# Copies for shuffles and a later iota in a sliding-window kernel bound by DMA

## The chip, the cores and the metric

One core of one Trainium2 chip. The time is the device time of one execution in microseconds (us). The kernel before takes 190.28 us (median of 3 runs, 190.25 to 190.29). The span of a profile, from its first to its last instruction, is about 1.7 us shorter than the time.

## The reference, cut to what matters

```python
# x: (16, 64, 64, 64) float32, window_size 8, stride 4  ->  n_h = n_w = 15
for i in range(n_h):
    for j in range(n_w):
        result[:, i, j] = x[:, :, 4*i:4*i+8, 4*j:4*j+8]     # (16, 64, 8, 8) each
```

It computes nothing: every window is copied out. The input has 16.8 MB, the output 3600 windows of 16 KB, 59 MB.

## The kernel before

The input stays in SBUF as `L`: 128 partitions, each one half of the channels of one batch element and one band of 16 image rows (4 bands). A tile `G` collects 128 windows of 16 KB, one in a partition, by copies of ScalarE and VectorE; GpSimd then scatters its rows to the output by an indirect DMA. Four `G` buffers rotate. A **crossing unit** fills one half of the partitions with windows that lie within a band (`s` = 2) and the other half with windows that cross into the next band (`s` = 3). The last band has no crossing windows, so 16 of the 128 rows fall outside the output and are dropped.

```python
    def fill(g, half, s, j, lo, n, copies):
        ...
            if s < NSLOT - 1:
                copy(out=g[d, cs, :, :], in_=L[f, :, s * ST : s * ST + WS, cols])
            else:
                copy(out=g[d, cs, 0:ST, :], in_=L[f, :, s * ST : RB, cols])
                nc.vector.stream_shuffle(out=g[d, cs, ST:WS, :], in_=L[f, :, 0:ST, cols], mask=nxt)

    def shf(out, in_):                       # an identity shuffle: a plain move
        nc.vector.stream_shuffle(out=out, in_=in_, mask=same)

    def mix(out, in_):
        k = out.shape[1] // 4
        act(out=out[:, 0:k], in_=in_[:, 0:k])
        shf(out=out[:, k:], in_=in_[:, k:])
    ...
            turn = crossed % 2               # in unit(), for s > 0
            crossed += 1
            fill(g, turn, s, j, 0, HP, (act, act))
            fill(g, 1 - turn, s + 1, j, 0, HP, (shf, mix))
            scatter(g, (idx_hi, idx_lo)[turn], j, s)
```

`turn` decides which half of the partitions gets the crossing windows. The iota and the index arithmetic stand ahead of the loads. At the end, two half tiles (the last column of windows) leave by DMAs of SyncE and ScalarE.

Of the kernel before, what the change touches and what calls it, by code (L numbers as in the profile page):

```python
# [10 lines left out]
def kernel(  # L11
# [7 lines left out]
    nc = tc.nc  # L19
    P = nc.NUM_PARTITIONS  # L20

    B, C, H, W = x.shape
# [8 lines left out]
    CH = 2  # L31
    HQ = P // (B * CH)
    CL = C // CH
# [4 lines left out]
    HP = P // CH  # L38
    YB = 8
    NY = B // YB  # L40
# [8 lines left out]
    L = lpool.tile([P, CL, RB, W], f32)  # L49
# [4 lines left out]
    SMALL, HWP = 4, 8  # L54

    def load(eng, ch, y, q, c0, c1):
        p0 = ch * HP + y * QP + q
        eng.dma_start(out=L[p0 : p0 + QP - HQ + 1 : HQ, c0:c1, :, :], in_=x_v[ch, y, q, :, c0:c1, :])  # L58
# [3 lines left out]
    def itile(name):  # L62
        return ipool.tile([P, 1], i32, name=name)

    pi, tb, tq, tc_, th, idx, idx_y0, idx_y1, idx_lo, idx_hi = (
        itile(n) for n in ("pi", "tb", "tq", "tc", "th", "idx", "idx_y0", "idx_y1", "idx_lo", "idx_hi")
    )
    FAR = float(2 * B * NWIN)
    nc.gpsimd.iota(pi[:, :], pattern=[[0, 1]], base=0, channel_multiplier=1)  # L69

    def bits(d, shift, mask):
        nc.vector.tensor_scalar(out=d[:, :], in0=pi[:, :], scalar1=shift, scalar2=mask, op0=ALU.logical_shift_right, op1=ALU.bitwise_and)  # L72
# [4 lines left out]
    def tt(d, a, b, op):  # L77
        nc.vector.tensor_tensor(out=d[:, :], in0=a[:, :], in1=b[:, :], op=op)  # L78
# [20 lines left out]
    tt(idx_lo, tb, th, ALU.add)  # L99
    mul(th, tc_, NW)  # L100
    tt(idx_lo, idx_lo, th, ALU.add)


    EC = 8
    x_b = x.rearrange("b (ch cl) (hq r) w -> ch hq b cl (r w)", ch=CH, hq=HQ)
    nc.scalar.dma_start(out=L[HP : HP + (B - 1) * HQ + 1 : HQ, 0:EC, :, :], in_=x_b[1, 0, :, 0:EC, :])

    for y in range(NY):
        for q in range(HQ):
            hw = y * HQ + q < HWP  # L110
            if hw:
                load(nc.sync, 0, y, q, SMALL, CL)
            load(nc.gpsimd, 0, y, q, 0, SMALL if hw else CL)
            load(nc.gpsimd, 1, y, q, EC if q == 0 else 0, CL)

    o_v = out.rearrange("b i j c r w -> (b i j) (c r w)")
    nxt = [min(p + 1, 31) for p in range(32)]
# [9 lines left out]
    def scatter(g, ix, j, s):  # L127
        st = nc.gpsimd.indirect_dma_start(  # L128
            out=o_v,
            out_offset=bass.IndirectOffsetOnAxis(ap=ix[:, 0:1], axis=0),  # L130
            in_=g.rearrange("p c r w -> p (c r w)"),
            in_offset=None,
            element_offset=(s * NW + j) * CFREE,
            bounds_check=B * NWIN - 1,
            oob_is_err=False,
        )
        free(st)

    def fill(g, half, s, j, lo, n, copies):

        d = slice(half * HP + lo, half * HP + lo + n)
        cols = slice(j * ST, j * ST + WS)
        for ch in (half, 1 - half):
            f = slice(ch * HP + lo, ch * HP + lo + n)
            cs = slice(ch * CL, (ch + 1) * CL)
            copy = copies[ch != half]
# [6 lines that stand above are left out]
    act, dve = nc.scalar.copy, nc.vector.tensor_copy  # L153
    same = list(range(32))


    def shf(out, in_):
        nc.vector.stream_shuffle(out=out, in_=in_, mask=same)  # L158

    def mix(out, in_):  # L160
        k = out.shape[1] // 4
        act(out=out[:, 0:k], in_=in_[:, 0:k])  # L162
        shf(out=out[:, k:], in_=in_[:, k:])


    EARLY = 3
# [2 lines left out]
    def tile_():  # L169
        nonlocal at  # L170
        at += 1
        return G[(at - 1) % NG]
# [16 lines left out]
    def unit(j, s, fast=False):  # L189
        nonlocal crossed  # L190
        g = tile_()
        if s == 0:
            fill(g, 0, 0, j, 0, HP, (act, dve if fast else shf))
            fill(g, 1, 1, j, 0, HP, (act, dve if fast else mix))
            scatter(g, idx, j, s)
        else:

            turn = crossed % 2
            crossed += 1
            fill(g, turn, s, j, 0, HP, (act, act))  # L200
            fill(g, 1 - turn, s + 1, j, 0, HP, (shf, mix))
            scatter(g, (idx_hi, idx_lo)[turn], j, s)

    for n in range(EARLY):
# [3 lines left out]
    for n in range(EARLY):  # L208
        part(1, 2 * n)
        unit(*plain.pop(0), fast=True)  # L210
    while plain:
        for w in cross[:3]:
            unit(*w)
        cross = cross[3:]
        unit(*plain.pop(0))


    j = NW - 1
    tile_()
    for s in range(2):  # L220
        g = tile_()
# [44 lines left out]
```

## Time and profile before

| | before |
|---|---|
| time, median | 190.28 us |
| VectorE, ScalarE, GpSimd busy | 75%, 74%, 25% |
| DMA, mean over the span | 401 GB/s |
| stores by GpSimd | 29, issued from 43 to 173 us |
| last crossing store lands; last DMA lands | 177.5 us; 187.6 us |

From the page: the summary by engine, then two rows of 40 slices (DMA share in tenths, GB/s), then one DMA queue (packets, MB, share of 16 engines).

```profile
DVE 142.5 (75%) x200; ACT 139.2 (74%) x89; POOL 46.9 (25%) x50
...
DMA  4999999999999999999999999999999999999993
GB/s 118 308 409 397 402 401 397 397 403 394 427 434 420 435 434 416 434 434 413 437 437 408 439 430 420 423 437 416 427 413 434 428 409 430 406 437 378 427 389 153
...
q14 instruction: 4, 0.03, 0.0%
```

DMA is full from the second slice to the last but one. The row `q14` looks like nothing: four packets of 8 KB, on a queue that the page calls `instruction`.

### The profile page before, as it was taken

To read this page: it belongs to the slowest core of one execution; us is meant where nothing else is said; L and a number is where in the kernel's file an instruction comes from. 1 tells how busy PE (TensorE), PEld (TensorE's weight loads), DVE (VectorE), ACT (ScalarE), POOL (GpSimd) and SP (SyncE) were. 2 spreads that over 40 slices of the span, in tenths; PEclk is the share of its full clock that TensorE was granted. 3 is DMA by queue.
4 is the path that set the end of the run, shared out by engine and by line. 5 is a ranking of instruction groups with operands and counts; after the bars stand their busy time and mean duration, and the time that the engine had idled before them with its cause. 6 is when DMAs were issued, how large, how long until landed. Compare 5 with 4: busy or idle time off the path is not lost.

```text
span 189.0 us, 557 instructions
## 1 busy us (share of the span) xinstructions
DVE 142.5 (75%) x200; ACT 139.2 (74%) x89; POOL 46.9 (25%) x50
## 2 busy tenths in 40 slices
DVE  4000009999697979799989999999999999997410
ACT  0000009998699999988889999999999999974740
POOL 7321212207217170522220222222222222223000
DMA  4999999999999999999999999999999999999993
GB/s 118 308 409 397 402 401 397 397 403 394 427 434 420 435 434 416 434 434 413 437 437 408 439 430 420 423 437 416 427 413 434 428 409 430 406 437 378 427 389 153
DMA packets 11044, 75.81 MB, mean 401 GB/s; under 512 B 3344, under 2 KB 3344, under 8 KB 7440
## 3 DMA queue, kind: packets, MB, share of 16 engines
q0 software_dynamic: 8784, 65.81, 84.0%
q1 hardware_dynamic: 2048, 8.91, 12.0%
q10 hardware_dynamic: 208, 1.05, 1.8%
q14 instruction: 4, 0.03, 0.0%
HBM read 16.78 MB, written 62.91 MB: 422 GB/s over the span
## 4 chain that ended last, share of the span: by engine, by line
DMA 66%; DVE 18%; issue 6%; ACT 3%; POOL 2%; DVEq 0%; ACTq 0%; PEldq 0%
DMA out_dram<-G,idx_hi 24%; DMA L<-in_x_dram 23%; DMA out_dram<-G,idx 13%; DVE G L158 10%; DMA out_dram<-G,idx_y 7%; DVE G L151 5%; DVE G L181 3%; ACT G L227 2%; POOL L L58 2%; ACT G L148 1%; DVE G L148 0%; DVEq L181 0%; POOL pi L69 0%; DVEq L158 0%; PEldq L261 0%
## 5 line engine op out<-in xcount | busy, mean ns | idle before, releaser
L148 ACT COPY G<-L 64x2048 f32<-64x2048 f32 x46 | 87.2, 1896 | 5.5 <-DMA out_dram<-G,idx 2.3
L181 DVE COPY G<-L 32x2048 f32<-32x2048 f32 x30 | 36.6, 1221 | 29.3 <-DMA L<-in_x_dram 26.7
L158 DVE STREAM_SHUFFLE G<-L 64x1024 f32<-64x1024 f32 (+3 forms) x40 | 55.7, 1392 | 1.3
L151 DVE STREAM_SHUFFLE G<-L 64x1024 f32<-64x1024 f32 x30 | 38.5, 1282 | 0.0
L181 ACT COPY G<-L 32x2048 f32<-32x2048 f32 x18 | 33.9, 1896 | 2.9 <-DMA L<-in_x_dram 2.3
L181 ACT ACT_TABLE_LOAD x1 | 1.3, 1283 | 28.3 <-DMA L<-in_x_dram 28.3
L58 POOL DMA_DIRECT2D L<-in_x_dram x16 | 10.9, 691 | 23.0 <-DMA L<-in_x_dram 22.5
L128 POOL DMA_INDIRECT out_dram<-G,idx_y x6 | 10.0, 1664 | 25.5 <-DVE G L181 24.5
L128 POOL DMA_INDIRECT out_dram<-G,idx x8 | 11.3, 1412 | 19.9 <-DVE G L158 6.5
L128 POOL DMA_INDIRECT out_dram<-G,idx_hi x8 | 7.7, 963 | 30.7 <-DVE G L151 23.1
L128 POOL DMA_INDIRECT out_dram<-G,idx_lo x7 | 6.7, 961 | 27.5 <-DVE G L151 19.1
L227 ACT COPY G<-L 32x2048 f32<-32x2048 f32 x4 | 7.6, 1896 | 5.1 <-DMA out_dram<-G,idx_lo 4.0
L162 ACT COPY G<-L 64x256 f32<-64x256 f32 (+1 forms) x20 | 9.1, 456 | 0.5
L227 DVE COPY G<-L 32x2048 f32<-32x2048 f32 x4 | 4.9, 1219 | 3.5 <-DMA out_dram<-G,idx_hi 2.4
L148 DVE COPY G<-L 64x2048 f32<-64x2048 f32 x6 | 7.3, 1222 | 0.2
L158 DVE LOAD_MASK_SELECT G<-L x40 | 0.4, 9 | 2.1 <-DMA out_dram<-G,idx_y 1.2
L72 DVE TENSOR_SCALAR tb<-pi 128x1 int32<-128x1 int32 x1 | 0.2, 153 | 1.0 <-POOL pi L69 1.0
L78 DVE TENSOR_TENSOR th<-tc,tq 128x1 int32<-128x1 int32 x2 | 0.3, 156 | 0.0
L75 DVE TENSOR_SCALAR th<-tc 128x1 int32<-128x1 int32 x2 | 0.3, 154 | 0.0
L69 POOL IOTA pi<- 128x1 int32 x1 | 0.1, 124 | 0.4 <-PEq L261 0.4
L151 DVE LOAD_MASK_SELECT G<-L x30 | 0.2, 7 | 0.0
L78 DVE CUSTOM_DVE_ANT_0 idx_lo<-tb,th 128x2 uint16<-128x2 uint16 x1 | 0.2, 159 | 0.0
(18 smaller groups left out, 2.6 us busy)
## 6 DMA issues: line engine op xcount, KB each, us to landing
L<-in_x_dram SPq DMA_DIRECT2D x8, 896.0 KB
L<-in_x_dram POOLq DMA_DIRECT2D x6, 1024.0 KB, 21.6
L<-in_x_dram POOLq DMA_DIRECT2D x2, 768.0 KB, 18.3
out_dram<-G SPq DMA_DIRECT2D x6, 256.0 KB
L<-in_x_dram POOLq DMA_DIRECT2D x8, 128.0 KB, 21.6
L<-in_x_dram ACTq DMA_DIRECT2D x1, 512.0 KB
out_dram<-G ACTq DMA_DIRECT2D x2, 256.0 KB
out_dram<-G,idx POOLq DMA_INDIRECT x8, 12.3
```

What stands on the lines that cost most here:

```text
L58: eng.dma_start(out=L[p0 : p0 + QP - HQ + 1 : HQ, c0:c1, :, :], in_=x_v[ch, y, q, :, c0:c1, :])
L69: nc.gpsimd.iota(pi[:, :], pattern=[[0, 1]], base=0, channel_multiplier=1)
L72: nc.vector.tensor_scalar(out=d[:, :], in0=pi[:, :], scalar1=shift, scalar2=mask, op0=ALU.logical_shift_right, op1=ALU.bitwise_and)
L75: nc.vector.tensor_scalar(out=d[:, :], in0=a[:, :], scalar1=float(m), scalar2=None, op0=ALU.mult)
L78: nc.vector.tensor_tensor(out=d[:, :], in0=a[:, :], in1=b[:, :], op=op)
L128: st = nc.gpsimd.indirect_dma_start(out=o_v, out_offset=bass.IndirectOffsetOnAxis(ap=ix[:, 0:1], axis=0), in_=g.rearrange("p c r w -> p (c ...
L148: copy(out=g[d, cs, :, :], in_=L[f, :, s * ST : s * ST + WS, cols])
L151: nc.vector.stream_shuffle(out=g[d, cs, ST:WS, :], in_=L[f, :, 0:ST, cols], mask=nxt)
L158: nc.vector.stream_shuffle(out=out, in_=in_, mask=same)
L162: act(out=out[:, 0:k], in_=in_[:, 0:k])
L181: (act if (2 * d + ch) % 3 == 0 else dve)(out=g[d * QP : (d + 1) * QP, ch * CL : (ch + 1) * CL, :, :], in_=L[f : f + QP, :, s * ST : s * S ...
L227: copy(out=g[d, ch * CL : (ch + 1) * CL, :, :], in_=L[f, :, s * ST : s * ST + WS, cols])
```

## The change

Its intent: start GpSimd's loads without the iota ahead of them, and free VectorE, which is full from 98 to 172 us (72.67 of 74 us busy), by moving plain rows with copies where identity shuffles stood (in this trace a shuffle of 2048 elements takes 2428 ns and a copy 1221).

```diff
-    nc.gpsimd.iota(pi[:, :], pattern=[[0, 1]], base=0, channel_multiplier=1)
+    EC = 8                      # this block moves up from behind the index arithmetic
+    ...
+            load(nc.gpsimd, 1, y, q, EC if q == 0 else 0, CL)
+            if y == 0 and q == 1:
+                nc.gpsimd.iota(pi[:, :], pattern=[[0, 1]], base=0, channel_multiplier=1)
 ...
-    def mix(out, in_):
+    def mix(out, in_, rest=shf):
         k = out.shape[1] // 4
         act(out=out[:, 0:k], in_=in_[:, 0:k])
-        shf(out=out[:, k:], in_=in_[:, k:])
+        rest(out=out[:, k:], in_=in_[:, k:])
+
+    def mixc(out, in_):
+        mix(out, in_, dve)
 ...
-            fill(g, 1 - turn, s + 1, j, 0, HP, (shf, mix))
+            fill(g, 1 - turn, s + 1, j, 0, HP, (dve, mixc))
```

More of the change, by code (lines that the diff above doesn't have):

```diff
@@ L68 @@
     FAR = float(2 * B * NWIN)
-    nc.gpsimd.iota(pi[:, :], pattern=[[0, 1]], base=0, channel_multiplier=1)
+    EC = 8
+    x_b = x.rearrange("b (ch cl) (hq r) w -> ch hq b cl (r w)", ch=CH, hq=HQ)
+    nc.scalar.dma_start(out=L[HP : HP + (B - 1) * HQ + 1 : HQ, 0:EC, :, :], in_=x_b[1, 0, :, 0:EC, :])
+    for y in range(NY):
+        for q in range(HQ):
+            hw = y * HQ + q < HWP
+            if hw:
+                load(nc.sync, 0, y, q, SMALL, CL)
+            load(nc.gpsimd, 0, y, q, 0, SMALL if hw else CL)
+            load(nc.gpsimd, 1, y, q, EC if q == 0 else 0, CL)
+            if y == 0 and q == 1:
+                nc.gpsimd.iota(pi[:, :], pattern=[[0, 1]], base=0, channel_multiplier=1)
     def bits(d, shift, mask):
@@ L101 @@
     tt(idx_lo, idx_lo, th, ALU.add)
-    EC = 8
-    x_b = x.rearrange("b (ch cl) (hq r) w -> ch hq b cl (r w)", ch=CH, hq=HQ)
-    nc.scalar.dma_start(out=L[HP : HP + (B - 1) * HQ + 1 : HQ, 0:EC, :, :], in_=x_b[1, 0, :, 0:EC, :])
-    for y in range(NY):
-        for q in range(HQ):
-            hw = y * HQ + q < HWP
-            if hw:
-                load(nc.sync, 0, y, q, SMALL, CL)
-            load(nc.gpsimd, 0, y, q, 0, SMALL if hw else CL)
-            load(nc.gpsimd, 1, y, q, EC if q == 0 else 0, CL)
     o_v = out.rearrange("b i j c r w -> (b i j) (c r w)")
```

## The prediction

> **What bounds the kernel now.** I began with the page's summary: VectorE 75% busy, ScalarE 74%, GpSimd 25%, and a DMA row that reads 9 in all slices but the first and the last. No engine is the bound over the whole span; the DMA engines may be. So I asked next for the stretches of the run, each with busy time by engine, DMA share (packet time as a share of 16 engines) and GB/s:
>
> ```profile
> core 0: us, DVE busy (x) ACT busy (x) POOL busy (x), PEclk, DMA share, GB/s
> 0.00:6.00 6.00, 2.34 (x20) 0.00 (x0) 4.84 (x13) 1.00 0.56 137
> 6.00:28.00 22.00, 0.00 (x0) 0.00 (x0) 4.05 (x7) 1.00 1.03 393
> ...
> 78.00:98.00 20.00, 18.64 (x30) 17.01 (x13) 3.86 (x5) 1.00 1.02 432
> ...
> 98.00:172.00 74.00, 72.67 (x111) 67.98 (x48) 15.38 (x16) 1.00 1.01 423
> 172.00:184.00 12.00, 4.88 (x4) 7.58 (x4) 1.58 (x1) 1.00 0.95 400
> ```
>
> The DMA share is about 1.0 from 6 us to 172 us. VectorE is full too from 98 to 172 us (72.67 of 74 us). Two resources that are both full need a tie-break, and that is the queue between them. The chain of waits shows it: each store's time from its issue by GpSimd to its landing.
>
> ```profile
> 83.59 14.00 DMA out_dram<-G,idx_hi
> ...
> 121.62 11.57 DMA out_dram<-G,idx_hi
> ...
> 144.96 10.68 DMA out_dram<-G,idx_hi
> ...
> 168.17 9.34 DMA out_dram<-G,idx_hi
> ```
>
> One 16 KB packet of a store takes 611 ns (median of the packets between 50 and 100 us), so 16 engines carry at most 16 x 16384 B / 611 ns = 429 GB/s. A crossing unit writes 112 rows (16 of its 128 fall outside the output), 7 for each engine, 7 x 0.611 = 4.28 us; a plain unit 128 rows, 8 x 0.611 = 4.89 us. A landing time of 14.0 us is some three stores in the queue, 9.34 us still two. VectorE makes units more slowly than DMA can carry them, so the backlog shrinks, but **it is not gone when the last unit is issued at 172.5 us**. VectorE being late therefore cost DMA almost nothing, and that decides the prediction.
>
> The production rate, from the timeline's issues by GpSimd near the end (153.93, 158.66, 163.41, 168.17, 172.51): 4.73, 4.75, 4.76 us for three crossing units and 4.34 for a plain one, 18.58 us for a group of four. DMA needs 3 x 4.28 + 4.89 = 17.73 us for the same group.
>
> The other part of the change lies at the start, read from the timeline:
>
> ```profile
> 0.74 0.69 ACTq L106 DMA_DIRECT2D L<-in_x_dram  x1
> 0.74 26.46 SPq L58 DMA_DIRECT2D L<-in_x_dram  x8
> 0.84 0.12 POOL L69 IOTA pi<- 128x1 int32 x1 [0.39 <-PEq L261]
> ...
> 1.48 4.99 POOL L58 DMA_DIRECT2D L<-in_x_dram  x8 [0.52 <-issue]
> ```
>
> GpSimd's first load starts at 1.48 us, 0.64 us after the iota started: 0.12 of iota and 0.52 of "issue", a gap in which it waited for nothing shown. The two hardware queues start at 0.74 us. In the packet records GpSimd's queue moves its first packets at about 4.5 us; until then the hardware queues move only some 200 GB/s, against about 400 once GpSimd's has joined.
>
> [...]copies of 2048 take 1221 to 1222 ns, shuffles 2428. [...]GpSimd's scatters take 0.96 us beside shuffles, but 1.86 to 2.50 us between 55 and 76 us, where VectorE copies. Yet DMA carried 428.6 GB/s from 50 to 78 us, packet bytes by time, as much as anywhere.[...]
>
> **The change, part by part.** The groups by form are needed here, as the mean of the page mixes shapes:
>
> ```profile
> L151 DVE STREAM_SHUFFLE G<-L 64x1024 f32<-64x1024 f32 x30 | 38.5, 1282 | 0.0
> ...
> L158 DVE STREAM_SHUFFLE G<-L 64x1024 f32<-64x1024 f32 x15 | 19.2, 1283 | 0.5
> L158 DVE STREAM_SHUFFLE G<-L 64x768 f32<-64x768 f32 x15 | 15.0, 999 | 0.5
> ```
>
> 1. Copies for shuffles. In each of 15 crossing units one 64x1024 and one 64x768 identity shuffle (the two rows of L158) become copies; the two real shuffles (L151) stay, and so do plain units. I estimate the copies from durations here. Shuffles of 1024 and 2048 elements, 1283 and 2428 ns, lie on 138 ns + 1.118 ns per element. With the same fixed part a copy of 2048 in 1221 ns gives 0.529 ns per element: 1024 take 680 ns, 768 take 544 ns. Saved in a unit: (1283 - 680) + (999 - 544) = 1058 ns. VectorE's cycle falls from 4.75 to some 3.7 us, its busy time from 142.5 by 15 x 1.06 = 15.9 to about 126.6 us.
> ScalarE's cycle in a crossing unit is two copies of 1.90, one of 0.40 and gaps, 4.27 us (155.72 to 159.99 in the timeline), unchanged. The slowest stage is then DMA at 4.28, with ScalarE level. On the path: from 98 to 172 us DMA moves at 423.5 GB/s in place of the 428 or so that it reached with a deeper queue. If all comes back, 74 x (1 - 423.5/428) = 0.8 us. I credit 0.5, because I can't see that the slightly longer packets there (618 ns against 611 near the end) come from the shallower queue at all.
> 2. The tail. From 172 to 184 us DMA moves 400 GB/s: up to 12 x (1 - 400/428) = 0.8 us. But at 177.55 us, when the buffer of the last half tile comes free, 4.2 MB are still to land, 9.8 us at 428 GB/s, and DMA ends 9.5 us later at 187.0. It is nearly gapless already. I credit 0.1 us.
> 3. The iota. GpSimd's first four loads start up to 0.64 us earlier, or only 0.12 if the gap of 0.52 belongs to the first load. I take 0.5. An earlier join is worth the missing half of the rate: 0.5 x 200/400 = 0.25 us, all of it on the path, since DMA is full from then on. The indices come some 3 us later, about 4 to 7 us, and the first scatter needs them at 43.3 us: no cost.
> 4. The cost: copies delay scatters. A unit's scatter is built while VectorE is on the next unit, whose first operation is the 0.68 us copy; so a scatter may go from 0.96 to 1.6 us. With two to three stores queued, this comes out of the backlog and not out of the end. I count 0.
>
> Sum: 0.5 + 0.1 + 0.25 = 0.85, rounded up to 1.0 as the two credits are cautious: 190.28 - 1.0 = 189.3 us.
>
> **Rivals.** *VectorE is the true bound.* For it: 98% busy for 74 us, and long pieces of the chain on L158 and L151. Four groups of four units would then shorten from 18.58 to 17.73 us or, with ScalarE's pace, a little less: 4 x 0.85 = 3.4 us, some 186.9 us. Against it: DMA's share of 1.01 in the same stretch. Time can't be taken out of a full pipe; the surplus would be a longer queue, landing times of 13 to 14 us at the end in place of 9.3. [...]each of 15 scatters 0.6 to 1.5 us later, at worst 9 to 22 us. Against it: the stretch from 55 to 76 us has denser copies, scatters of up to 2.50 us and a full DMA. A weak form, a few tenths lost at the tail where only two stores are queued, stays possible: 190.3 to 190.6. *The start is hidden.* If the first software packets wait for something else than their issue, part 3 gives nothing: 189.5 us.
>
> **Range and chances.** Even if all stores went at 429 GB/s, the 139 us from 48 to 187 us (at 424 on average) would shrink by 1.6 us, with 0.3 at the start 1.9: 188.4 is the floor. The top, 190.2, is a gain eaten by scatters. Faster by over 2% needs under 186.5, below that floor: 2%. Slower by over 2% needs DMA to run dry for 4 us: 1%.
>
> **What would show it.** Right: GpSimd's first load before 1.1 us; copies of about 0.68 and 0.54 us and VectorE near 127 us busy; issue-to-landing times that stay at 12 us or more to the end; DMA from 98 us on near 428 GB/s; VectorE and ScalarE now waiting for landings. Wrong: if DMA moves clearly more than 429 GB/s, or if its share falls below 0.95 in the middle with scatters over 2 us, my account of queue[...] fails.

Cut where marked, here and in the expectations below, is what no trace or run of this case shows. The rival of which the figures "each of 15 scatters 0.6 to 1.5 us later" remain is that VectorE's copies delay GpSimd's scatters until DMA runs dry; the delays are estimates from the trace's 0.96 us beside shuffles, 2.50 us beside copies and the 0.68 us worked out for a copy.

## The result

The changed kernel takes **191.11 us** (median of 6 runs, 190.77 to 191.37) against 190.28 (190.11 to 190.60, 6 runs): ratio 1.0041, 95% interval 1.0027 to 1.0055. It is slower by 0.8 us, well outside the noise, and above the predicted range, though within 2% as forecast. A ratio here is the mean time of one kernel's runs over that of the other's of the same rounds, so it isn't quite the ratio of the medians quoted.

The page of the changed kernel, same rows:

```profile
DVE 127.7 (68%) x170; ACT 139.2 (74%) x89; POOL 48.0 (25%) x50
...
DMA  4999999999999999999999999999999999999883
GB/s 122 347 404 400 400 400 398 400 398 398 441 430 409 435 444 406 430 440 416 444 420 414 439 440 406 437 420 420 437 409 427 423 416 414 440 395 437 381 350 156
```

VectorE lost 14.8 us of work and the time went up. The DMA row shows 8 in two slices near the end, where before it showed 9.

The groups by form, for the moves in the crossing units (L152: real shuffles; L151 and L165: the new copies):

```profile
L152 DVE STREAM_SHUFFLE G<-L 64x1024 f32<-64x1024 f32 x30 | 38.3, 1277 | 0.0
...
L151 DVE COPY G<-L 64x1024 f32<-64x1024 f32 x15 | 10.3, 689 | 8.0 <-DMA out_dram<-G,idx_hi 3.9 <-DMA out_dram<-G,idx_y 2.1 <-DMA out_dram<-G,idx 1.1
...
L165 DVE COPY G<-L 64x768 f32<-64x768 f32 x15 | 8.3, 555 | 0.5
```

The copies take what was worked out (689 and 555 ns for 680 and 544), and VectorE now waits for stores to land (8.0 us at L151).

The chain of waits (start, us, what), to be set against 14.00, 11.57, 10.68 and 9.34 us before:

```profile
92.10 13.62 DMA out_dram<-G,idx_hi
...
119.64 12.81 DMA out_dram<-G,idx_hi
...
163.84 14.08 DMA out_dram<-G,idx_hi
177.92 0.02 issue
...
178.00 1.91 ACT G L232
```

The queue stays deep to the end, as predicted (12.2 to 14.2 us from issue to landing for every store issued after 119 us). But look at where the last crossing store lands: it is issued at 163.84 in place of 168.17 us, 4.3 us earlier, and lands at 177.92 in place of 177.51, later. The last half tile can start only then (its buffer comes free). The stretches tell the same:

```profile
98.00:172.00 74.00, 60.44 (x86) 67.57 (x48) 17.52 (x17) 1.00 1.01 424
172.00:184.00 12.00, 4.88 (x4) 7.58 (x4) 0.00 (x0) 1.00 0.90 378
184.00:189.00 5.00, 0.00 (x0) 0.00 (x0) 0.00 (x0) 1.00 0.40 164
```

From 98 to 172 us the rate is 424 GB/s (423 before): no gain. From 172 to 184 it is 378 (400 before): a loss. One caution: these two profiles are of executions that took 190.74 us (before) and 190.77 us (after), so between them they hardly show the 0.8 us; r1 and r2 below are a pair that does.

The start, from the timeline:

```profile
1.38 2.63 POOL L58 DMA_DIRECT2D L<-in_x_dram  x4 [0.93 <-PEq L266]
4.08 0.17 POOL L83 IOTA pi<- 128x1 int32 x1
4.15 2.42 POOL L58 DMA_DIRECT2D L<-in_x_dram  x4
```

GpSimd's first load starts at 1.38 in place of 1.48 us. Nearly all of the gap ahead of it belonged to the first load and not to the iota.

### Sixteen landings in place of one

A store has not one landing in the trace but 16, at different moments; I take them for one of each of the 16 DMA engines that the page counts. The wait that the chain shows ends with the last of them (177.92 us for the last crossing store of the changed kernel, in the chain and in the landings alike). Here are two stores in a row of the changed kernel around 160 us: issue and last landing (us), and how far ahead of the last engine the other fifteen were.

```
issue 145.77, last 158.74: -2.49 -2.48 -2.47 -2.42 -2.39 -2.37 -2.32 -2.31 | -0.60 -0.53 -0.33 -0.27 -0.24 -0.21 -0.17 0
issue 151.42, last 164.62: -3.43 -3.43 -3.42 -3.39 -3.32 -3.31 -3.25 -3.25 | -1.37 -1.30 -1.08 -1.03 -0.99 -0.97 -0.83 0
```

Two things stand out, in every profile of the kernel before and of the changed one. First, **the 16 engines are two groups of eight**, and one is some 3 us ahead from the first store on (first engine to last: 3.0 us before, 2.8 after). Second, between these two stores **one engine falls back alone** by about 0.8 us against the rest of its group; the last landings are 5.88 us apart where 4.85 is usual for a store of 128 rows. In between lies a packet of the queue `instruction`: at 159.83 us, 8 KB in 309 ns. I call such packets fetches, of instructions, by the queue's name. On the chain of packets that it stands in (each begins where the one before ends, so I take them for one engine's), the 16 KB packet after it takes 956 ns and the last but one before it 971 ns, where 611 is usual (the one directly before it takes 613). (360 + 309 + 345) ns = 1.01 us is what this engine lost. An engine falls back alone near 62 us in both kernels too, and near 146 us before the change; near 62 us only the packet after the fetch is that long (960 and 951 ns).

These fetches I take for VectorE's, by a count of instructions (the packets don't name their engine). In the kernels run here they come when VectorE has run 61 to 63 and then 192 to 198 of its recorded instructions (r14 and r15 below, with 189 in all, have the first alone; r6, with 103 more, has three, at 90, 196 and 319). The copies have no LOAD_MASK_SELECT ahead of them as the shuffles have (70 of these before, 40 after), so VectorE runs 30 instructions fewer (170 for 200), and its second fetch comes at 160 in place of 146 us.

### The profile page after: what moved, and what is told of

Same layout as the page of the kernel before. It is cut to its first block, busy times and chain, and to the rows that moved or that the text cites. A ratio compares the mean times of both kernels' runs of the same rounds, so it can differ in the third digit from the quotient of the medians. Undisturbed runs are those within 1.5% of the kernel's fastest.

```text
span 189.0 us, 527 instructions
## 1 busy us (share of the span) xinstructions
DVE 127.7 (68%) x170; ACT 139.2 (74%) x89; POOL 48.0 (25%) x50
## 3 DMA queue, kind: packets, MB, share of 16 engines
q1 hardware_dynamic: 2048, 8.91, 11.9%
## 4 chain that ended last, share of the span: by engine, by line
DMA 75%; DVE 15%; ACT 2%; POOL 2%; issue 2%; DVEq 0%; ACTq 0%; POOLq 0%; PEldq 0%
DMA out_dram<-G,idx_hi 28%; DMA out_dram<-G,idx 21%; DMA out_dram<-G,idx_y 14%; DMA L<-in_x_dram 12%; DVE G L186 11%; ACT G L232 2%; POOL L L58 2%; DVE G L160 2%; DVE G L151 1%; DVE G L149 0%; ACT G L149 0%; DVEq L186 0%; POOL pi L83 0%; DVE G L152 0%; POOLq L83 0%
## 5 line engine op out<-in xcount | busy, mean ns | idle before, releaser
L186 DVE COPY G<-L 32x2048 f32<-32x2048 f32 x30 | 36.6, 1221 | 25.9 <-DMA L<-in_x_dram 22.7
L152 DVE STREAM_SHUFFLE G<-L 64x1024 f32<-64x1024 f32 x30 | 38.3, 1277 | 0.0
L160 DVE STREAM_SHUFFLE G<-L 64x2048 f32<-64x2048 f32 (+1 forms) x10 | 21.6, 2162 | 0.2
L151 DVE COPY G<-L 64x1024 f32<-64x1024 f32 x15 | 10.3, 689 | 8.0 <-DMA out_dram<-G,idx_hi 3.9
L129 POOL DMA_INDIRECT out_dram<-G,idx_hi x8 | 8.9, 1112 | 25.7 <-ACT G L164 25.7
L165 DVE COPY G<-L 64x768 f32<-64x768 f32 x15 | 8.3, 555 | 0.5
L152 DVE LOAD_MASK_SELECT G<-L x30 | 0.2, 7 | 0.0
```

The lines of the kernel that those rows point to most:

```text
L129: st = nc.gpsimd.indirect_dma_start(out=o_v, out_offset=bass.IndirectOffsetOnAxis(ap=ix[:, 0:1], axis=0), in_=g.rearrange("p c r w -> p (c ...
L165: rest(out=out[:, k:], in_=in_[:, k:])
L186: (act if (2 * d + ch) % 3 == 0 else dve)(out=g[d * QP : (d + 1) * QP, ch * CL : (ch + 1) * CL, :, :], in_=L[f : f + QP, :, s * ST : s * S ...
```

## The experiments

I had two theories at first. *Straggler*: the end is set by the slowest of 16 DMA engines; what the change does to that engine decides. *Port* (the name that the expectations use; no view shows a port): VectorE's copies hold up GpSimd's stores or their packets. What the trace before shows of it: GpSimd's scatters took 0.96 us beside shuffles, and 1.86 to 2.50 us between 55 and 76 us, where VectorE copies. "Slow packets" below are 16 KB packets of the stores that take 680 to 800 ns, between 50 and 180 us (median of all: 613 to 614 ns in the first two profiles). "Lands" is the last landing of the last crossing store, which frees the buffer of the last half tile.

| run | time, us | before, us | ratio (95%) | last VectorE fetch, us | slow packets | lands, us |
|---|---|---|---|---|---|---|
| before, first profile | 190.28 | | 1 | 146.6 | 11 | 177.5 |
| after, first profile | 191.11 | 190.28 | 1.0041 (1.0027, 1.0055) | 159.8 | 57 | 177.9 |
| r1 before again | 190.44 | 190.58 | 0.9992 (0.9979, 1.0006) | 146.1 | 4 | 177.6 |
| r2 after again | 191.43 | 190.58 | 1.0043 (1.0029, 1.0057) | 160.3 | 53 | 178.4 |
| r3 iota only | 190.43 | 190.58 | 0.9995 (0.9981, 1.0008) | 146.4 | 4 | 177.4 |
| r4 copies only | 191.22 | 190.58 | 1.0031 (1.0017, 1.0045) | 160.3 | 50 | 178.4 |
| r5 after, copies split | 190.81 | 190.41 | 1.0024 (1.0011, 1.0038) | 146.4 | 49 | 178.0 |
| r6 before, fetches moved | 191.39 | 190.41 | 1.0062 (1.0049, 1.0076) | 159.8 | 8 | 178.5 |
| r7 after, halves swapped | 189.83 | 190.41 | 0.9975 (0.9962, 0.9989) | 159.3 | 51 | 176.8 |
| r8 after, no skipped buffer | 191.69 | 190.41 | 1.0069 (1.0055, 1.0083) | 160.2 | 50 | 178.3 |
| r9 after, at the old pace | 190.59 | 190.36 | 1.0012 (1.0000, 1.0024) | 148.6 | 12 | 177.7 |
| r10 before, less work | 191.09 | 190.36 | 1.0035 (1.0023, 1.0047) | 160.3 | 58 | 178.4 |
| r11 before, halves swapped | 189.46 | 190.36 | 0.9954 (0.9942, 0.9966) | 144.7 | 16 | 176.2 |
| r12 iota only, halves swapped | 189.47 | 190.36 | 0.9953 (0.9940, 0.9965) | 145.0 | 30 | 176.6 |
| r13 before, max for shuffle | 190.84 | 190.45 | 1.0020 (1.0006, 1.0034) | 159.9 | 10 | 178.0 |
| r14 after, fewer instructions | 194.76 | 190.45 | 1.0227 (1.0213, 1.0241) | 81.3 | 152 | 181.4 |
| r15 r14, halves swapped | 193.35 | 190.45 | 1.0156 (1.0142, 1.0169) | 81.1 | 161 | 180.0 |

All are correct but r10, which is wrong on purpose.

### r1 and r2: both kernels once more

No edit.

> The kernel before, unchanged, for a second profile and for the noise. 190.3 us, ratio 1.000 within 0.2%. Straggler theory (the end is set by the slowest of the 16 DMA engines, the one that also fetches VectorE's instructions): in the store phase that engine's landings again show two jumps of 0.2 to 0.5 us against the other slow engines, near 63 and 150 us, because it has 0.4 to 0.7 us in hand before each fetch. Port theory: nothing to say.

> The changed kernel, unchanged, for a second profile. 191.1 us, ratio 1.004. Straggler theory: the eight slow engines are bunched within 0.3 us at the first store, so the two fetches (near 62 and 160 us) push the last landing back by 0.6 and 1.0 us. If this second profile shows no such jumps at a time of 191 us, the theory falls.

The times repeat, and this pair of profiles (executions of 190.44 and 191.28 us) shows the loss where the first pair could not: the last crossing store lands at 177.55 us in r1 and at 178.43 in r2, 0.88 us later, and the stretch from 172 to 184 us has 406 and 384 GB/s:

```profile
172.00:184.00 12.00, 4.88 (x4) 7.58 (x4) 1.48 (x1) 1.00 0.96 406
...
172.00:184.00 12.00, 4.88 (x4) 7.58 (x4) 0.00 (x0) 1.00 0.91 384
```

The first form of the straggler theory fell in part: in r1 the slow eight were bunched within 0.5 us at the first store, the two fetches set the last landing back by about a full microsecond each, and the kernel still was as fast as before. (In r2 they were bunched within 0.6 us, where 0.3 was expected.) So the spread of the engines at the first store isn't what differs between the kernels. What differs is when the fetch comes: in r1 at 146 us, and by the last crossing store the straggler has made up 0.6 of its 1.0 us lag (0.99 us behind the next engine at its landing at 147.5, 0.41 at 177.6). In r2 it comes at 160 us, and it makes up 0.4 (0.83 to 0.43), while the bunched group ahead of the fetch had been slow already: from 142 to 159 us its landings came 4.99, 3.81, 5.00 and 3.75 us apart, where 4.84 to 4.88 and 3.65 are usual.

### r3 and r4: the parts apart

```diff
 r3 = the changed kernel with
-            fill(g, 1 - turn, s + 1, j, 0, HP, (dve, mixc))
+            fill(g, 1 - turn, s + 1, j, 0, HP, (shf, mix))
 r4 = the kernel before with the same line the other way, and mixc
```

> Only the iota moved; shuffles as before. Straggler theory: the earlier loads gain about 0.6 us but bunch the slow engines, so the fetches cost some 1.0 us more than before: 190.6 to 191.0. Port theory[...]: the gain of the start alone remains, 189.7 to 190.0, clearly faster than before.

> Only the copies in place of the shuffles; the iota first as before. Straggler theory: the slow engines are as spread at the first store as before, so the fetches cost what they cost before: 190.1 to 190.4, ratio 0.999 to 1.001. Port theory: all of the loss stays here and the gain of the start is missing: 191.3 to 191.7, ratio 1.006 or more.

The iota does nothing that five rounds could show (0.9995). Both expectations for r3 are missed: it is faster than the 190.6 us that the straggler theory set as the least, and slower than the 190.0 us that the port theory set as the most. The copies carry the loss (1.0031). That speaks for the port theory's side of r4, though at 191.22 us and 1.0031 it lies below the 191.3 to 191.7 and 1.006 that it expected. Both theories had to be told apart by what else the copies change: the pace of production and the number of instructions.

### r5 and r6: the fetch moved

```diff
 r5 = the changed kernel with
+    def dve2(out, in_):
+        k = out.shape[1] // 2
+        dve(out=out[:, 0:k], in_=in_[:, 0:k])
+        dve(out=out[:, k:], in_=in_[:, k:])
     def mixc(out, in_):
-        mix(out, in_, dve)
+        mix(out, in_, dve2)
 ...
-            fill(g, 1 - turn, s + 1, j, 0, HP, (dve, mixc))
+            fill(g, 1 - turn, s + 1, j, 0, HP, (dve2, mixc))
 r6 = the kernel before with
+    pad = ipool.tile([P, 1], f32, name="pad")
+    for _ in range(103):
+        nc.vector.memset(pad[:, :], 0.0)
```

> The changed kernel with each plain copy of the crossing units cut in two, so that VectorE runs as many instructions as before the change, and its second instruction fetch should come near 146 to 150 us again in place of 160. Theory A (a fetch near the end costs the straggling DMA engine its whole 0.9 us, an earlier one is half made up): 190.4 to 190.8, ratio at most 1.002. Theory B (copies as such[...] slow the store packets): the loss stays, 191.1 to 191.5.

> The kernel before with 103 tiny memsets of VectorE ahead of the index arithmetic, where it idles for the loads. They shift its instruction stream so that the last fetch should come near 160 us (and one more falls in the load phase, the other near 84 us). No copy is changed. Theory A: the loss appears without the change, 190.9 to 191.5. Theory B: 190.4 to 190.7, as before. If the shift misses 160 us, this run says nothing about A.

r5 brings the fetch back to 146 us and regains about half (1.0024), with as many slow packets as the change. r6 shows the loss, and more, without a single copy in the crossing units; but a third fetch came in during the loads (10.4 us), and the straggler was 0.8 us behind already at the first store. It shows that fetches cost, not what moving one costs.

### r7 and r8: what sets the end

```diff
 r7 = the changed kernel with
-            turn = crossed % 2
+            turn = (crossed + 1) % 2
 r8 = the changed kernel with
     j = NW - 1
-    tile_()
     for s in range(2):
```

> The changed kernel with the halves swapped in every crossing unit, so that of 15 units the slow eight engines get seven with 8 rows and eight with 6 in place of eight and seven. If the slow group of engines sets the end, it has two packets of 0.61 us less: 1.2 us faster, 189.8 to 190.2. If the end is set by the copies and waits of the tail, or by DMA as a whole, nothing: 191.0 to 191.5.

> The changed kernel without the skipped buffer ahead of the last two half tiles, so that they start in buffers that come free 4 us earlier. If the chain landing, copies, store of the tail sets the end: 1 to 2 us faster, 189 to 190.2. If the slowest DMA engine sets it (it has 16 packets left when the waited-for tile lands, 9.8 us, which is all of the tail): no gain, 191.0 to 191.5.

r7 settles the groups. In the traces of both kernels the lead of the fast eight jumps by 1.2 us (two packets of 0.611 us) in one crossing unit and back in the next (2.8, 3.9, 2.6 and 3.8 us at the landings from 92 to 106 us of the changed kernel), as it must if each group of eight serves one half of the partitions and the dropped rows lie in the one half and then the other. That reading foretold the 1.2 us of r7. Of 15 units, eight gave the fast group the short share. With one more short share for the slow group, the kernel has a ratio of 0.9975 where the change has 1.0041, some 1.2 to 1.3 us less, and beats the kernel before.

r8 lets the last two half tiles start some 3 and 4 us earlier (169.91 and 173.75 us for 173.17 and 178.00), and gains nothing. When the last crossing store lands, its slowest engine still has, by an equal share of rows, 16 packets of 16 KB to move, 8 of the last plain store and 8 of the half tiles: 16 x 0.611 = 9.8 us, an estimate. The last DMA lands 9.7 to 10.1 us after it in r1 to r13 and in the first two profiles, so that engine can have had hardly a gap. The tail looks like a chain of wait, copy and store; it is one engine working off its list. (That r8 is 0.3% slower than the change isn't explained.)

### r9 and r10: the pace without the copies, the copies without the pace

```diff
 r9 = the changed kernel with, at the end of each crossing unit,
+            h = slice((1 - turn) * HP, (2 - turn) * HP)
+            shf(scr[h, :, :, :], g[h, turn * CL : turn * CL + 24, ST:WS, :])   # into a scratch tile
 r10 = the kernel before with, in the crossing units,
-            fill(g, 1 - turn, s + 1, j, 0, HP, (shf, mix))
+            fill(g, 1 - turn, s + 1, j, 0, HP, (shf, part_of_mix))     # mix without its shuffle
```

> The changed kernel with one useless 64x768 shuffle into a scratch tile at the end of each crossing unit: VectorE copies as in the change, but makes units no faster than before (4.7 us) and runs 30 instructions more, so the fetch is back near 146 us. Depth and fetch theory (faster production keeps the queue deep and the fetch late; both cost, the copies themselves don't): the slow packets (over 680 ns, some 50 after 130 us) vanish, 190.3 to 190.6. Port theory[...]: the slow packets stay and with them at least half of the loss, 190.8 to 191.3.

> Wrong result on purpose. The kernel before without the 64x768 shuffle of each crossing unit: no copy of VectorE there, but a production as fast as in the changed kernel (3.7 us) and as few instructions, so a late fetch near 160 us and a deep queue. Depth and fetch theory: it is as slow as the changed kernel though it does less, 191.0 to 191.5, with some 50 slow packets. Port theory: it is as fast as before or faster, 189.8 to 190.4, without slow packets.

This speaks against the port theory. r10 has no copy in the crossing units, and less work than the kernel before, and it is as slow as the change within the intervals, with 58 slow packets. Its groups by form show GpSimd's scatters at their shortest, 961 ns, as beside shuffles before:

```profile
L128 POOL DMA_INDIRECT out_dram<-G,idx_hi x8 | 7.7, 961 | 26.0 <-ACT G L162 26.0
...
L128 POOL DMA_INDIRECT out_dram<-G,idx_lo x7 | 6.7, 961 | 24.4 <-ACT G L162 24.4
```

And its chain shows the same deep queue as the change, 14.21 us from issue to landing at the end:

```profile
164.21 14.21 DMA out_dram<-G,idx_hi
178.43 0.02 issue
```

r9 has the copies, at the old pace and with the fetch at 149 us: 12 slow packets, and a loss of 0.12%, at the edge of what can be told from zero. So it is **making units faster, and with fewer instructions, that costs**, not how they are made. Which of the two costs, r9 and r10 can't tell: each changes the pace and the fetch together.

### r11 and r12: a version that beats both

```diff
 r11 = the kernel before, r12 = r3, each with
-            turn = crossed % 2
+            turn = (crossed + 1) % 2
```

> The kernel before with the halves swapped in the crossing units (as in r7): the slow group of engines has two packets of 0.61 us less. 189.1 to 189.4, ratio 0.994, faster than r7 because the shuffles' shallower queue and earlier fetch remain.

> As r11, with the iota behind four loads as in the change. The iota showed no clear gain alone (ratio 0.9995): the same as r11 within 0.15%, 188.9 to 189.4; beyond that the iota would matter once the slow engines are relieved.

Both beat both kernels: 189.46 and 189.47 us, 0.5% below before. That is a little less than expected (0.994; both lie just above the 189.4 us set as the most). The stretches of r11 show the gain where it should be, 418 GB/s from 172 to 184 us in place of 400:

```profile
98.00:172.00 74.00, 72.03 (x111) 67.15 (x48) 15.37 (x17) 1.00 1.01 425
172.00:184.00 12.00, 4.92 (x4) 7.58 (x4) 0.83 (x1) 1.00 0.99 418
184.00:189.00 5.00, 0.00 (x0) 0.00 (x0) 0.00 (x0) 1.00 0.19 75
```

VectorE is as busy as ever; nothing was sped up. The work of the two groups of engines was evened out. Note the slow packets: 16 in r11 and 30 in r12, at the old pace and with a shallow queue, and no difference in time between the two. Slow packets are thus no measure of the loss, and don't need a deep queue.

### r13, r14, r15: fetch and depth apart

```diff
 r13 = the kernel before with, for the identity shuffles of the crossing units,
+        nc.vector.tensor_tensor(out=out, in0=in_, in1=in_, op=ALU.max)
 r14 = the changed kernel with that max for the plain units' shuffles, and all index
       arithmetic but the four bit extractions by nc.gpsimd in place of nc.vector
 r15 = r14 with turn = (crossed + 1) % 2
```

> The kernel before with the plain rows of the crossing units moved by a max of the input with itself (exact, [...]without a mask load): production as before, 30 instructions fewer, so the last fetch near 160 us with a shallow queue. If the late fetch alone costs: 0.4 us more than before, 190.7 to 191.0, ratio 1.002 to 1.003, with few slow packets. If only the depth costs: 190.3 to 190.5, ratio within 1.001.

> The changed kernel with some 26 VectorE instructions fewer (most index arithmetic on GpSimd after its loads, the plain units' shuffles as max of the input with itself), so that VectorE's second fetch doesn't come before the end; pace and queue as in the change. If the late fetch costs the straggler its 0.8 to 1.0 us: 190.2 to 190.5, ratio at most 1.001, and no jump of a lone engine near 160 us. If depth alone costs: 191.0 to 191.4.

> As r14 with the halves swapped. If the two gains add: r7 (ratio 0.9975) less some 0.7 us, 189.0 to 189.3, ratio 0.993 to 0.995, level with or better than r11 and r12. If the fetch is no cost: 189.8, as r7.

r13 is the cleanest one: nearly the old pace, no added fetch, 30 instructions fewer, fetch at 160 us, and only 10 slow packets. It loses 0.20%. In its trace the straggler is still 0.68 us behind the next engine when the last crossing store lands (178.03 us); in the four profiles with the old pace and the fetch at 146 to 149 us (before, r1, r3, r9) it is 0.03 to 0.41 us, with that landing at 177.4 to 177.7 us. One thing else did change: beside the max, the scatters took longer than the 0.96 us beside shuffles.

```profile
L161 DVE TENSOR_TENSOR G<-L 64x1024 f32<-64x1024 f32 x15 | 18.3, 1220 | 2.1 <-DMA out_dram<-G,idx_y 1.0 <-DMA out_dram<-G,idx_hi 0.5 <-DMA out_dram<-G,idx 0.2
...
L128 POOL DMA_INDIRECT out_dram<-G,idx_hi x8 | 9.7, 1212 | 26.6 <-ACT G L148 13.3 <-DVE G L151 13.3
```

r9, whose scatters in these units took 1.08 to 1.14 us and whose fetch is early, lost 0.12%. By time alone the two can't be told apart (1.0020 and 1.0012, each known to 0.12 to 0.14%); that r13's loss is the fetch's rests on the landings as well.

r14 and r15 failed as tests of time: GpSimd took 1.0 to 1.2 us for most of the small index operations (128x1 int32), as the timeline shows, where VectorE took 0.14 to 0.16 us before, so its first scatter came at 47.42 in place of 43 us.

```profile
42.09 1.13 POOL L92 TENSOR_TENSOR idx<-tb,th 128x1 int32<-128x1 int32 x1
43.30 1.17 POOL L92 TENSOR_TENSOR idx_y<-idx_y,idx 128x1 int32<-128x1 int32 x1
...
47.42 1.13 POOL L130 DMA_INDIRECT out_dram<-G,idx_y  x1 [0.18 <-issue]
```

They still show three things. Swapping the halves gains there too (0.7%). No engine falls back alone near 160 us when no fetch comes there. And all 16 engines landed the first store within 0.15 us of each other; slow packets then appear from 50 us on, 152 of them.

## Why the prediction was wrong

It forecast a gain of 1.0 us, and the change lost 0.8. Point by point, by its own steps.

*What bounds the kernel* was right in the large: DMA, not VectorE; the surplus of units became a longer queue, and the rival with VectorE as the bound, 186.9 us, fell. It was wrong in the picture of DMA: "so 16 engines carry at most 16 x 16384 B / 611 ns = 429 GB/s" treats them as one pipe. The step fails here. A buffer comes free, and the kernel ends, when the **slowest** engine is done. One group of eight is some 3 us ahead and has nothing to do at the end; the mean share of 1.01 hides that until the last 15 us.

*Part 1*, "I credit 0.5" us for the return to 428 GB/s: the sizes of the copies were right, the credit was wrong. The rate stayed at 424 GB/s: the deep queue did not make packets faster. With it came some 50 slow packets, in the changed kernel and in r10 alike, where the unswapped kernels at the old pace have 4 to 12.

*Part 2*, the tail, 0.1 us: the sign was wrong. DMA carried 378 GB/s there in place of 400. The fast eight ran further ahead (5.1 us at the last store of GpSimd against 2.9) and stopped earlier, and the slow engine's list ended no earlier. The reading behind the term shows the same error: at 177.55 us not 4.2 MB were left but 3.5 to 3.7, as the fast eight had already moved part of theirs. At 428 GB/s that is 8.3 to 8.7 us and not 9.8, so the tail of 9.5 us was "nearly gapless" for the slow eight only.

*Part 3*, the iota, 0.25 us: the term mis-sized is the 0.5 us of an earlier load. It measured 0.10 us, and r3 gives no gain that five rounds can show. The first profiles seemed to show more (landings 0.7 us earlier); r1 and r2 show that as much differs between two profiles of one kernel. The "missing half" of the rate was misread as well: GpSimd's packets start at 4.5 us, but DMA still moves 197 GB/s from 4.5 to 6 us and 336 from 6 to 8.

*Part 4*, "I count 0" for the copies' delay of the scatters: right for that delay, as r10 shows the loss without any copy; the scatters of the crossing units took 1.11 and 0.99 us in the mean beside the copies, not 1.6, and 0.96 before. But no term stood for what fewer instructions and a faster pace do to the slowest engine. Two are measured. A late fetch costs about 0.2%: r13 against before (+0.20%), and r5 against the change (1.0024 against 1.0041; those intervals overlap, so r13 is the better witness, with the reservation made there). A deep queue with the fetch left early costs about as much again: r5 against before (+0.24%). Together 0.4%, which is the change's 1.0041 to 1.0043. That the effects add up is read from these four cells, each known to about 0.14% either way. With the halves swapped, the faster pace and the late fetch together cost 0.2% (r7 at 0.9975 against r11 at 0.9954), which these intervals can't tell from 0.4%.

Of the rivals, "a weak form, a few tenths lost at the tail where only two stores are queued" came nearest in size, but not in cause.

Two smaller slips: the mean rate from 48 to 187 us was 420 to 421 GB/s and not 424, so the floor of its range stood a microsecond too high; and the sum of 0.85 was rounded up to 1.0 on no measurement. Of its signs of being right, the copies' times, VectorE's busy time and waits and the deep queue came, the earlier first load and 428 GB/s didn't; neither of its signs of being wrong came. It had no sign for a slowest engine.

**What stays open.** What a slow packet waits for is in no view. In the changed kernel 40 of the 57 are among the last three 16 KB packets of a store and 14 among the first two, on the slow eight where the group can be told. They come after 130 us when the queue is deep, and from 50 us on in r14, where all engines are bunched; r12, where the swap brings the two groups closer, has 30 with a shallow queue. So bunched engines in one another's way is my reading, and it is argued, not shown. That a straggler makes up some of its lag after a fetch is measured; that it does so because it runs out of step with its group is argued too. Which engine a packet ran on is inferred: the records carry no engine number, and I chained packets by one ending where the next begins. Where the lead of 3 us at the first store comes from was not looked into; in r14, where DMA falls to 244 GB/s in the slice ahead of the first stores, it is absent and builds up later (3.4 us at the last crossing store).

## What to carry to other kernels

When DMA is the bound, ask for the slowest of the 16 engines before asking for more work in the queue: compare their landings of one store, and even out what each half of the partitions sends (swapping the halves gained 0.5% in r11). Freeing an engine that feeds a full queue gained nothing here, and cost (1.0041; r10 1.0035). In this kernel, tuned to a few tenths of a per cent, even the number of instructions mattered: one of the engines that carry the data lost 1.0 us beside a fetch of 8 KB in the changed kernel, and with VectorE's last fetch at 160 in place of 146 us the kernel took 0.2% longer (r13, with the reservation made there).
